# Five layer borders: the next layer's first two units of weights token-major behind the last product

## The chip, the cores and the metric

One of the cores of a Trainium2 chip runs the whole program, in one launch. The metric is the time of the program on the device in microseconds (us). The engines of a core have a queue each and run it in order: TensorE (PE: matmuls, PEld: its weight loads), VectorE (DVE), ScalarE (ACT), GpSimd (POOL), and SyncE (SP), which here issues the loads of weights.

## The reference, cut to what matters

A chain of layers over 256 tokens of width 1024, in fp32: two layers of mixers with a feed-forward each (the first dense, the second 8 experts of which a token takes 2), then forgetting attention, a conv FFN, a sparse attention, and another conv FFN. Each takes the normalised sum of all before it.

```python
h = rms_norm(x, norm_mix_g[layer]) * (1.0 + scale_m) + shift_m
... = jnp.split(h @ w_in[layer], split_points, axis=-1)      # four mixers
x = x + gate_m * mixed
h = rms_norm(x, norm_ffn_g[layer]) * (1.0 + scale_f) + shift_f
y = swiglu(h, w1, w3, w2)                                     # (silu(h @ w1) * (h @ w3)) @ w2
x = x + gate_f * y
...
def conv_ffn(xn, w_up, conv_w, conv_b, w_down):
    u = xn @ w_up
    c = sum((conv_w[j] * u_pad[:, j:j + T] for j in range(CONV_W)), conv_b)   # over tokens
    gate, val = jnp.split(c, 2, axis=-1)
    return (jax.nn.silu(gate) * val) @ w_down
```

## The kernel before, in words

**Products.** Every fp32 value is held as two parts, hi (rounded to fp32r) and lo (the rest); a product is three matmuls (mm3: hi·hi, lo·hi, hi·lo, lines L404 to L406). The features of a layer stand in hTh and hTl, feature-major: 8 pieces of 128 features by 256 tokens.

**Weights.** They come as a stream of units of 1 MB (`Stream`), in the order that `plan` writes down, 1024 x 256 or 256 x 1024 values each. SP loads a unit into one of 6 raw tiles; each half is split by a ScalarE cast (hi, L250) and a VectorE subtraction (lo, L251) into one of 4 split tiles, up to 3 halves ahead of their use. Some units are ada units: they are not split and belong to the modulation vectors of later layers. TensorE works through them in groups ("ada", "adt") that `fill` or `gap` puts in between, after the numbers in `FILL`.

**A unit of features.** `feat_unit` makes 256 new features by 256 tokens, 48 matmuls ("fu"). `tok_half` makes the same with tokens on the partitions, for 128 tokens at a time ("tu"), from a unit packed token-major; before, this is done for the first unit behind a border where the layer wants it so (mixers, forgetting and sparse attention).

**A border.** `close` is the last product of a layer: the output x, 256 tokens by 1024, in four quadrants (128 tokens tt by 512 columns n) of 12 matmuls each ("acc"). Behind each quadrant comes the residual (L1024 and L1025, with a gate at the first two borders, where GpSimd adds for tt = 0), the squares (L500), and behind the second one of each tt the norm (L428 to L435), the normalised rows xn (L487, or L492 and L490), their transposes on TensorE (`turned`, "tr", L447) and the features of the next layer (hTh by L468 or L473, hTl by L474). For tt = 0 this lies beside the second half of the last product. For tt = 1 TensorE runs 11 matmuls without a result behind the product (`warm`, L343) or, at the first two borders, an ada group, and then the transposes and the next layer's first units.

**Borders meant here.** B1: first mixers to dense FFN. B2: dense FFN to second mixers. B3: forgetting attention to conv FFN. B4: conv FFN to sparse attention. B5: sparse attention to conv FFN. (The border into the experts, `close_routed`, and the one out of them have code of their own.)

**FFN.** `gated_ffn` takes 11 pairs of units: for pair j a first and a second unit, then `pair` (swiglu, or the convolution over tokens and the gating: tile cf, 8 steps on VectorE, L1086 to L1094, then the split gh, gl), whose product with the down unit comes two pairs later.

## Time and profile before

| | |
|---|---|
| median of 3 runs | 2317.92 us (2312.59 to 2321.94) |
| profiled execution, its own time | 2317.72 us |
| its span, first to last instruction | 2315.6 us |
| PE busy | 2223.6 us (96%) |
| DVE busy | 1759.5 us (76%) |
| ACT busy | 1395.9 us (60%) |
| POOL busy | 90.3 us (4%) |
| mean granted clock of TensorE | 0.983 |

A share of busy time is a mean over stages. The experts take the middle of the span, from about 600 to 1590 us; the borders are short stretches at the ends of the other layers.

### The profile page before, as it was taken

To read this page: it belongs to the slowest core of one execution; us is meant where nothing else is said; L and a number is where in the kernel's file an instruction comes from. 1 tells how busy PE (TensorE), PEld (TensorE's weight loads), DVE (VectorE), ACT (ScalarE), POOL (GpSimd) and SP (SyncE) were. 2 spreads that over 40 slices of the span, in tenths; PEclk is the share of its full clock that TensorE was granted. 3 is DMA by queue.
4 is the path that set the end of the run, shared out by engine and by line. 5 is a ranking of instruction groups with operands and counts; after the bars stand their busy time and mean duration, and the time that the engine had idled before them with its cause. 6 is when DMAs were issued, how large, how long until landed. Compare 5 with 4: busy or idle time off the path is not lost. (4 is left out here: it accounts for less than half of the span.)

```text
span 2315.6 us, 34028 instructions
## 1 busy us (share of the span) xinstructions
PE 2223.6 (96%) x13353; PEld 1853.8 (80%) x13353; DVE 1759.5 (76%) x2279; ACT 1395.9 (60%) x1913; POOL 90.3 (4%) x118
## 2 busy tenths in 40 slices
PE   6998999899999999999999999898999998999999
PEld 4777888887887878787878878787879997778997
DVE  3665445586999899999999899886777776676776
ACT  3534334545777777777777777676655454455454
POOL 1000000001000000000000000001004001000000
PEclk8999999999999999999999999999999999999999
DMA  9757774635999999999999998794324544312542
GB/s 396 276 230 282 270 248 173 220 105 206 367 367 343 354 336 367 349 351 333 369 349 362 341 349 309 272 345 177 118 102 169 204 167 174 128 37 93 200 176 79
DMA packets 87559, 584.34 MB, mean 252 GB/s; under 512 B 9984, under 2 KB 11648, under 8 KB 20960
## 3 DMA queue, kind: packets, MB, share of 16 engines
q1 hardware_dynamic: 84096, 575.22, 67.2%
q0 software_dynamic: 1296, 4.59, 0.6%
q8 instruction: 106, 1.74, 0.3%
q10 hardware_dynamic: 2000, 2.29, 0.3%
q14 instruction: 61, 0.50, 0.1%
HBM read 580.76 MB, written 1.05 MB: 251 GB/s over the span
## 5 line engine op out<-in xcount | busy, mean ns | idle before, releaser
L251 DVE TENSOR_TENSOR lo<-raw,hi 128x1024 fp32r<-128x1024 f32 x711 | 853.2, 1227 | 280.7 <-ACT hi L250 274.0
L250 ACT CAST hi<-raw 128x1024 fp32r<-128x1024 f32 x718 | 740.2, 1049 | 356.8 <-PE fu L405 171.5
L404 PE MATMUL fu<-hTh,hi 128*128 128x256 f32 x1536 | 444.1, 289 | 4.4 <-DVE hTh L473 2.6
L406 PE MATMUL fu<-hTh,lo 128*128 128x256 f32 x1536 | 437.5, 285 | 2.2 <-DVE lo L251 2.2
L405 PE MATMUL fu<-hTl,hi 128*128 128x256 f32 x1536 | 437.8, 285 | 0.2 <-DVE hTl L474 0.2
L404 PE MATMUL h<-hi,xh 128*128 128x512 f32 x896 | 360.9, 403 | 6.2 <-DVEq L1418 6.0
L405 PE MATMUL h<-lo,xh 128*128 128x512 f32 x896 | 354.8, 396 | 4.6 <-DVE lo L251 4.6
L406 PE MATMUL h<-hi,xl 128*128 128x512 f32 x896 | 355.3, 397 | 0.0
L404 PEld LDWEIGHTS fu<-hTh,hi 128*128 128x128 f32 x1536 | 294.9, 192 | 21.3 <-issue 12.3
L405 PEld LDWEIGHTS fu<-hTl,hi 128*128 128x128 f32 x1536 | 293.3, 191 | 4.3 <-issue 3.2
L406 PEld LDWEIGHTS fu<-hTh,lo 128*128 128x128 f32 x1536 | 293.3, 191 | 2.8 <-DVE lo L251 2.8
L251 DVE TENSOR_TENSOR lo<-more,hi 128x1024 fp32r<-128x1024 f32 x216 | 258.3, 1223 | 21.4 <-ACT hi L250 19.7
L250 ACT CAST hi<-more 128x1024 fp32r<-128x1024 f32 x216 | 224.2, 1052 | 44.4 <-PE h L406 21.7
L405 PEld LDWEIGHTS h<-lo,xh 128*128 128x128 f32 x896 | 169.1, 189 | 45.6 <-DVE lo L251 7.9
L404 PEld LDWEIGHTS h<-hi,xh 128*128 128x128 f32 x896 | 168.9, 189 | 44.0 <-issue 6.4
L406 PEld LDWEIGHTS h<-hi,xl 128*128 128x128 f32 x896 | 168.8, 188 | 41.0
L404 PE MATMUL y<-hi,egh 128*128 128x512 f32 x448 | 177.1, 395 | 0.7 <-ACT egh L418 0.7
L406 PE MATMUL y<-hi,egl 128*128 128x512 f32 x448 | 177.6, 396 | 0.0
L405 PE MATMUL y<-lo,egh 128*128 128x512 f32 x448 | 176.5, 394 | 0.8 <-DVE lo L251 0.8
L404 PE MATMUL acc<-hi,gh 128*128 128x512 f32 x264 | 105.7, 400 | 0.0
L405 PE MATMUL acc<-lo,gh 128*128 128x512 f32 x264 | 104.7, 397 | 0.5 <-DVE lo L251 0.4
L406 PE MATMUL acc<-hi,gl 128*128 128x512 f32 x264 | 104.4, 396 | 0.0
(488 smaller groups left out, 2919.7 us busy)
## 6 DMA issues: line engine op xcount, KB each, us to landing
raw<-in_moe_dram SPq DMA_DIRECT2D x201, 1024.0 KB, 6.9
more<-in_moe_dram SPq DMA_DIRECT2D x108, 1024.0 KB, 7.0
raw<-in_w_ada_dram SPq DMA_DIRECT2D x48, 1024.0 KB, 6.8
raw<-in_f_up_dram SPq DMA_DIRECT2D x44, 1024.0 KB, 4.9
raw<-in_ffn_dram SPq DMA_DIRECT2D x33, 1024.0 KB, 5.2
row<-in_moe_dram SPq DMA_DIRECT2D x54, 512.0 KB, 7.0
raw<-in_w_in_dram SPq DMA_DIRECT2D x24, 1024.0 KB, 6.7
raw<-in_f_dn_dram SPq DMA_DIRECT2D x22, 1024.0 KB, 5.6
```

Of the source, the lines that this page charges most:

```text
L250: self.nc.scalar.copy(hi, src)
L251: (self.nc.gpsimd if pool else self.nc.vector).tensor_tensor(lo, src, hi.bitcast(FT), op=OP.subtract)
L404: t.matmul(out, a[0], b[0], start=start, stop=False)
L405: t.matmul(out, a[0], b[1], start=False, stop=False)
L406: t.matmul(out, a[1], b[0], start=False, stop=stop)
```

## The change

At the five borders, the first two units of the next layer are made token-major (`early=2`): their weights are packed that way on the host, and their four halves are split during the last product, into work tiles of the layer that ends (`spare`, `spares`) and not into the four split tiles. ScalarE casts all four when `close` starts; VectorE subtracts two ahead of the first residual, one after the second quadrant and one after the third. Behind the last product TensorE does the first 128 tokens of the first unit and of half of the second, then the transposes of tt = 1, the other half of the second unit, and after the features of tt = 1 both units for these. `warm` is gone there. hTl of tt = 0 now stands ahead of the last residual on VectorE. GpSimd takes no part in a border any more (residual, hTl, one split). At the first two borders two ada groups stand in the close, one behind the product and one ahead of the second 128 tokens; `FILL` takes them from other places, 40 groups in all as before. The FFNs and the sparse attention copy the token-major units they need feature-major (`tok_copy`, 2 ScalarE copies a unit) and turn them with 4 transposes a unit (`tok_turn`, "tt"); in an FFN, pair 0 is gated in the middle of pair 1. The second mixers use both as they are.

```diff
+    def spare(self, pairs):
...
+        rest = []
...
+            for t, src in zip(hi, raw):
+                self.nc.scalar.copy(t, src)
+            rest.append(lambda hi=hi, lo=lo, raw=raw: [
+                self.nc.vector.tensor_tensor(l, src, t.bitcast(FT), op=OP.subtract) for l, src, t in zip(lo, raw, hi)])
+            self.parts[self.cut] = (hi, lo)
+            self.spared.add(self.cut)
+            self.cut += 1
+        return rest
...
-    FILL = [1, 1, 1, 1, 1, 1, 1, 2, 2, 2, 2, 1], [3], [1] * 17 + [0] * 5, [3], [1] + [0] * 11
+    FILL = [1, 1, 1, 1, 1, 1, 1, 2, 2, 2, 2, 1], [2, 2], [0] * 2 + [1] * 16 + [0] * 4, [2, 2], [0] * 12
...
-        sub = v if tt or shift is None else nc.gpsimd
         def rest():
             if late:
                 v.tensor_copy(hi, tmp)
-            sub.tensor_tensor(lo, tmp, hi.bitcast(FT), op=OP.subtract)
+            v.tensor_tensor(lo, tmp, hi.bitcast(FT), op=OP.subtract)
...
-                if tt and n:
+                if n:
                     self.nc.vector.tensor_scalar(xn[:, s], self.x[:, tt, s], r, None, op0=OP.mult)
...
+    def spares(self, n):
+        r = []
+        for size, m in self.spare:
+            for _ in range(min(m, n - len(r))):
+                if size == 8192:
+                    t = self.w([P, 2, D], "sp", FR)
+                    r.append(([t[:, 0]], [t[:, 1]]))
+                else:
+                    r.append(tuple([self.w([P, size // 4], "sp", FR) for _ in range(4096 // size)] for _ in range(2)))
+        assert len(r) == n
+        return r
...
+        early = then[2] if then else 0
+        s = self.s
+        lows = s.spare(self.spares(2 * early))
+        def low(n):
+            for _ in range(min(n, len(lows))):
+                lows.pop(0)()
+        low(2)
         for tt in range(2):
             for n in range(2):
                 for i, (g, half, first, last) in enumerate(items):
                     if then and tt and n and i == m:
-                        rest = self.turned(0, rows[0][1], then)
+                        for f in self.turned(0, rows[0][1], then):
+                            f()
                     self.down_half(acc, g, half, first, last, tt, n)
                 self.residual(acc, gate, tt, n, rows[tt][1] if then else None)
                 if not then:
                     t, c = slice(tt * P, (tt + 1) * P), slice(n * 512, (n + 1) * 512)
                     self.nc.sync.dma_start(self.out[t, c], self.x[:, tt, c])
-                for f in rest:
-                    f()
                 if then:
                     self.summed(tt, rows[tt], n)
+                    if tt + n == 1:
+                        low(1)
+                    assert not (lows and tt and n)
             if then and tt == 0:
                 self.scaled(0, rows[0], then)
         if then:
             self.scaled(1, rows[1], then)
-            self.s.ahead(1, not (gap and then[2]))
-            if gap:
-                with self.s.quiet():
-                    gap()
-            else:
-                self.warm(11)
-            if then[2]:
-                self.s.ahead(2)
-            rest = self.turned(1, rows[1][1], then)
-            if then[2]:
-                with self.s.quiet():
-                    self.tok_half(0)
+            with s.quiet():
+                gap()
+                self.tok_half(0, 0)
+                if early > 1:
+                    self.tok_half(0, 1, (0,))
+                rest = self.turned(1, rows[1][1], then)
+                if early > 1:
+                    self.tok_half(0, 1, (1,))
+                gap()
             for f in rest:
                 f()
-            if then[2]:
-                self.tok_half(1)
-            else:
-                self.s.ahead(2)
+            s.ahead(4)
+            for u in range(early):
+                self.tok_half(1, u)
         return rows
...
-    def tok_half(self, tt):
+    def tok_half(self, tt, u=0, parts=(0, 1)):
         hi, lo = self.hT
-        if tt == 0:
-            self.first = [self.ps("tu"), self.ps("tu")]
-            self.firsts = [t.rearrange("p (k c) -> p k c", k=4) for h in self.s.halves(2) for t in h]
-            self.s.pinned = 2
-        s = slice(tt * P, (tt + 1) * P)
-        for j in range(8):
-            wh, wl = self.firsts[j // 4 * 2:][:2]
-            self.mm3(self.first[tt][:, :256], (hi[:, j, s], lo[:, j, s]), (wh[:, j % 4], wl[:, j % 4]), j == 0, j == 7)
+        s = self.s
+        if tt == 0 and 0 in parts:
+            if u == 0:
...
+            self.firsts.append((s.halves(2), held))
+            s.pinned += held
+            self.first.append([self.ps("tu"), self.ps("tu")])
+        halves, held = self.firsts[u]
+        t = slice(tt * P, (tt + 1) * P)
+        for h in parts:
+            wh, wl = ([p.rearrange("p (k c) -> p k c", c=256) for p in (w if isinstance(w, list) else [w])] for w in halves[h])
+            for k in range(4):
+                j = 4 * h + k
+                i, c = divmod(k, 4 // len(wh))
+                self.mm3(self.first[u][tt][:, :256], (hi[:, j, t], lo[:, j, t]), (wh[i][:, c], wl[i][:, c]), j == 0, j == 7)
         if tt:
-            self.s.pinned = 0
+            s.pinned -= held
+    def tok_copy(self, ps):
+        t = self.w([P, 2, 256], "tk")
+        for tt in range(2):
+            self.nc.scalar.copy(t[:, tt], ps[tt][:, :256])
+        return t
+    def tok_turn(self, t):
+        ps = self.ps("tt")
+        for m in range(2):
+            for tt in range(2):
+                self.nc.tensor.transpose(ps[:, (2 * m + tt) * P:(2 * m + tt + 1) * P], t[:, tt, m * P:(m + 1) * P],
+                                         self.cc("ident"))
+        return ps
...
-        (eng or (v if tt or gate is None else self.nc.gpsimd)).tensor_tensor(self.x[:, tt, s], t, self.x[:, tt, s], op=OP.add)
+        (eng or v).tensor_tensor(self.x[:, tt, s], t, self.x[:, tt, s], op=OP.add)
...
-        return (close or self.close)(acc, items, gate, then, gap)
-    def gated_ffn(self, pair, fill, gate, then, hT=None, gap=None):
-        acc = self.accs()
+        return close(acc, items, gate, then) if close else self.close(acc, items, gate, then, gap)
+    def gated_ffn(self, pair, fill, gate, then, hT=None, gap=lambda: None):
+        acc = None
         g = []
         n = 11
+        early = [self.tok_copy(ps) for ps in self.first]
         for j in range(n):
-            a = self.feat_unit()
+            if j == 0:
+                fill()
+                if len(early) == 2:
+                    fill()
+                    continue
+                b = self.feat_unit()
+                a = self.tok_turn(early.pop())
+            else:
+                a = self.feat_unit()
+                fill()
+                if early:
+                    g.append(pair(0, *map(self.tok_turn, early)))
+                    early = []
+                b = self.feat_unit()
             fill()
-            b = self.feat_unit()
-            fill()
+            if j == 2:
+                acc = self.accs()
             if j == n - 1:
                 g.append(pair(j, a, b))
...
-            nc.scalar.copy(vt[:, tt].rearrange("p b g d -> p (b g d)"), self.first[tt][:, :256])
-        ps = self.feat_unit()
+            nc.scalar.copy(vt[:, tt].rearrange("p b g d -> p (b g d)"), self.first[0][tt][:, :256])
         raw = self.w([P, 2, T], "raw")
-        nc.scalar.copy(raw.rearrange("p a t -> p (a t)"), ps)
+        nc.scalar.copy(raw.rearrange("p a t -> p (a t)"), self.tok_turn(self.tok_copy(self.first[1])))
...
-        self.phase("fox", c64=8, c1024=4, c1536=8, c2048=11, c8192=3)
-        self.forgetting(last, self.feats(self.row(a["fg"][0:1])))
+        self.phase("fox", c64=8, c1024=4, c1536=8, c2048=12, c8192=3, spare=((8192, 1), (2048, 3)))
+        self.forgetting(last, self.feats(self.row(a["fg"][0:1]), early=2))
...
-        ffn = dict(c64=8, c1024=4, c2048=20)
+        ffn = dict(c64=8, c1024=4, c2048=15, c8192=2, spare=((8192, 2), (2048, 2)))
         self.phase("cff0", **ffn)
-        rows = self.conv_ffn(0, self.feats(self.row(a["kvg"]), early=True), kT)
+        rows = self.conv_ffn(0, self.feats(self.row(a["kvg"]), early=2), kT)
...
-        self.phase("nsa", c64=12, c256=2, c512=6, c1024=7, c1536=3, c2048=12, c4096=3)
-        self.sparse(rows, self.row(a["bg"]), hT, self.feats(self.row(a["fg"][1:2])))
+        self.phase("nsa", c64=12, c256=2, c512=6, c1024=7, c1536=3, c2048=12, c4096=3, spare=((4096, 1), (2048, 3)))
+        self.sparse(rows, self.row(a["bg"]), hT, self.feats(self.row(a["fg"][1:2]), early=2))
```

On TensorE at B3, before: the rows from the last filler to the first unit (tr: transposes of the rows xn; fu: first unit, feature-major; identb: the filler's operand).

```order
L343 MATMUL warm_16703<-identb 128x512
L447 MATMUL tr_16715<-consts,xn_16608 128x128 x4
L447 MATMUL tr_16721<-consts,xn_16608 128x128 x4
L404 MATMUL fu_16752<-hTh,hi 128x256
L405 MATMUL fu_16752<-hTl,hi 128x256
L406 MATMUL fu_16752<-hTh,lo 128x256
```

After, around the same transposes (tu: second unit token-major for tt = 0; sp: its split weights in spare tiles):

```order
L440 MATMUL tu_16778<-sp_16637,hTh 128x256
L441 MATMUL tu_16778<-sp_16639,hTh 128x256
L442 MATMUL tu_16778<-sp_16637,hTl 128x256
L483 MATMUL tr_16792<-consts,xn_16630 128x128 x4
L483 MATMUL tr_16798<-consts,xn_16630 128x128 x4
L440 MATMUL tu_16778<-sp_16640,hTh 128x256
L441 MATMUL tu_16778<-sp_16642,hTh 128x256
L442 MATMUL tu_16778<-sp_16640,hTl 128x256
```

The transposes now follow 36 matmuls of the next layer instead of fillers, and are followed by 12 more that don't need their result.

On VectorE at B3, before, from the third quadrant's residual to the second half's rows:

```order
L1025 TENSOR_TENSOR x<-acc_16434,x 128x512
L502 TENSOR_SCALAR st_16607<-st_16607 128x1
L1025 TENSOR_TENSOR x<-acc_16435,x 128x512
L474 TENSOR_TENSOR hTl<-tr_16668,hTh 128x4x128
L474 TENSOR_TENSOR hTl<-tr_16674,hTh 128x4x128
L430 TENSOR_SCALAR rm_16690<-st_16607 128x1
L431 TENSOR_SCALAR rm_16690<-rm_16690 128x1
L434 SCALAR_TENSOR_TENSOR rm_16690<-rm_16690 128x1
L435 SCALAR_TENSOR_TENSOR st_16607<-rm_16690 128x1
L487 SCALAR_TENSOR_TENSOR xn_16608<-x,st_16607,row_15268 128x512 x2
```

After, the same place (L284: a split into a spare tile; L1103 is the residual, L509 hTl, L522 the rows):

```order
L1103 TENSOR_TENSOR x<-acc_16456,x 128x512
L537 TENSOR_SCALAR st_16629<-st_16629 128x1
L284 TENSOR_TENSOR sp_16642<-raw,sp_16640 128x512
L284 TENSOR_TENSOR sp_16643<-raw,sp_16641 128x512
L509 TENSOR_TENSOR hTl<-tr_16717,hTh 128x4x128
L509 TENSOR_TENSOR hTl<-tr_16723,hTh 128x4x128
L1103 TENSOR_TENSOR x<-acc_16457,x 128x512
L466 TENSOR_SCALAR rm_16739<-st_16629 128x1
L467 TENSOR_SCALAR rm_16739<-rm_16739 128x1
L470 SCALAR_TENSOR_TENSOR rm_16739<-rm_16739 128x1
L471 SCALAR_TENSOR_TENSOR st_16629<-rm_16739 128x1
L522 SCALAR_TENSOR_TENSOR xn_16630<-x,st_16629,row_15290 128x512 x2
```

A split and hTl of tt = 0 now stand ahead of the last residual; three more splits stand further ahead, around the first residuals.

On VectorE behind B5, before, the end of pair 0's gating and the start of pair 1's:

```order
L1088 SCALAR_TENSOR_TENSOR cf_20621<-fu_20555,vecs,cf_20621 128x254
L1094 TENSOR_TENSOR cf_20614<-cf_20614,cf_20621 128x512
L416 CAST gh_20630<-cf_20614 128x512
L419 TENSOR_TENSOR gl_20631<-cf_20614,gh_20630 128x512
L251 TENSOR_TENSOR lo<-raw,hi 128x1024 x4
L1087 SCALAR_TENSOR_TENSOR cf_20752<-fu_20634,vecs,cf_20752 128x255
L1088 SCALAR_TENSOR_TENSOR cf_20752<-fu_20634,vecs,cf_20752 128x254
```

After, the same two gatings (tt: units turned from token-major):

```order
L1180 SCALAR_TENSOR_TENSOR cf_20736<-tt_20724,vecs,cf_20736 128x254
L1186 TENSOR_TENSOR cf_20729<-cf_20729,cf_20736 128x512
L452 CAST gh_20745<-cf_20729 128x512
L455 TENSOR_TENSOR gl_20746<-cf_20729,gh_20745 128x512
L267 TENSOR_TENSOR lo<-raw,hi 128x1024 x2
L1179 SCALAR_TENSOR_TENSOR cf_20808<-fu_20662,vecs,cf_20808 128x255
L1180 SCALAR_TENSOR_TENSOR cf_20808<-fu_20662,vecs,cf_20808 128x254
```

Two splits instead of four stand between the two gatings.

## Rows read from the trace of the kernel before

**Rows 1.** The page, busy time by engine (share of the span, instructions)

```profile
PE 2223.6 (96%) x13353; PEld 1853.8 (80%) x13353; DVE 1759.5 (76%) x2279; ACT 1395.9 (60%) x1913; POOL 90.3 (4%) x118
```

**Rows 2.** Waits of PE, 164 to 200 us: us, times, longest

```profile
PE tr L447 <- ACT xn L492: 3.2, 2, 2.6
PE fu L404 <- DVE hTh L473: 2.6, 1, 2.6
```

**Rows 3.** Waits of PE, 400 to 432 us

```profile
PE tr L447 <- ACT xn L492: 3.3, 2, 2.6
PE tu L405 <- DVE lo L251: 2.7, 2, 1.8
PE adt L711 <- ACT xn L708: 0.7, 1, 0.7
```

**Rows 4.** Waits of PE, 1930 to 1960 us

```profile
PE tr L447 <- DVE xn L487: 3.3, 2, 2.0
PE fu L404 <- ACT hi L250: 1.4, 1, 1.4
PE fu L406 <- DVE lo L251: 0.8, 1, 0.8
```

**Rows 5.** Timeline of PE, 1730 to 1753 us: start, length, what

```profile
1731.79 2.55 PE L343 MATMUL warm<-identb 128*128 128x512 bf16 x11
...
1739.07 0.56 PE L404 MATMUL fu<-hTh,hi 128*128 128x256 f32 x1
...
1744.05 0.28 PE L406 MATMUL fu<-hTh,lo 128*128 128x256 f32 x1
...
1751.85 0.28 PE L405 MATMUL fu<-hTl,hi 128*128 128x256 f32 x1
```

**Rows 6.** Windows: length, busy us by engine, PEclk (granted clock), DMA share, GB/s

```profile
186.20:190.80 4.60, 4.36 (x19) 4.09 (x20) 4.60 (x5) 2.43 (x3) 0.18 (x1) 0.50 0.84 264
412.50:416.00 3.50, 3.50 (x17) 3.50 (x18) 3.47 (x8) 1.62 (x4) 0.00 (x0) 0.53 0.98 407
1941.70:1945.40 3.70, 3.70 (x21) 3.70 (x20) 1.90 (x3) 1.87 (x2) 0.12 (x1) 0.54 0.69 229
1951.80:1955.50 3.70, 3.67 (x18) 3.67 (x19) 3.38 (x3) 1.56 (x2) 0.00 (x0) 0.55 0.39 102
2119.00:2123.00 4.00, 4.00 (x23) 3.98 (x21) 2.98 (x4) 3.42 (x4) 0.00 (x0) 0.57 0.00 0
28.35:31.82 3.47, 0.01 (x1) 0.00 (x0) 2.15 (x8) 3.02 (x7) 0.97 (x1) 0.80 1.00 409
33.00:37.00 4.00, 3.75 (x17) 3.75 (x18) 4.00 (x7) 1.39 (x5) 4.00 (x10) 0.50 0.93 348
423.00:431.00 8.00, 6.20 (x48) 5.45 (x47) 7.03 (x7) 3.64 (x5) 0.00 (x0) 1.00 0.62 228
```

**Rows 7.** Groups of DVE instructions, 164 to 190 us

```profile
L251 DVE TENSOR_TENSOR lo<-raw,hi 128x1024 fp32r<-128x1024 f32 x5 | 5.8, 1217 | 0.0
```

**Rows 8.** Groups of DVE instructions, 2100-2119 us: busy, mean ns, idle

```profile
L487 DVE SCALAR_TENSOR_TENSOR xn<-x,st,row 128x512 f32<-128x512 f32 x4 | 4.9, 1272 | 0.1
L1025 DVE TENSOR_TENSOR x<-acc,x 128x512 f32<-128x512 f32 x4 | 2.8, 690 | 3.2 <-PE acc L406 3.2
```

**Rows 9.** Timeline of DVE, 2131 to 2156 us

```profile
2131.69 0.48 DVE L1087 SCALAR_TENSOR_TENSOR cf<-fu,vecs,cf 128x255 f32<-128x255 f32 x1
...
2139.60 4.62 DVE L251 TENSOR_TENSOR lo<-raw,hi 128x1024 fp32r<-128x1024 f32 x4
2144.15 0.48 DVE L1087 SCALAR_TENSOR_TENSOR cf<-fu,vecs,cf 128x255 f32<-128x255 f32 x1
...
2151.22 4.62 DVE L251 TENSOR_TENSOR lo<-raw,hi 128x1024 fp32r<-128x1024 f32 x4
```

**Rows 10.** Waits of PE, 1753 to 1790 us

```profile
PE fu L406 <- DVE lo L251: 1.4, 2, 1.1
```

**Rows 11.** The page, DMA issues: KB each, us to landing

```profile
raw<-in_f_up_dram SPq DMA_DIRECT2D x44, 1024.0 KB, 4.9
```

More of the change, by code (lines that the diff above doesn't have):

```diff
@@ L38, in _ts1024, with _first256 @@
     return w.reshape(-1, 2, P, D).transpose(0, 2, 1, 3).reshape(-1, P, 2048)
+def _first256(w, *units):
+    r = _ws(w)
+    for u in units:
+        r[u] = _ts256(w[:, u * 256:(u + 1) * 256])[0]
+    return r
 def _kcol(w):
@@ L192, in pack @@
     w = a["f_w_up_2"]
-    o["f_up"] = np.stack([_ws(w[l]) for l in range(2)])
+    o["f_up"] = np.stack([_first256(w[l], *EARLY_UP) for l in range(2)])
     o["f_dn"] = np.stack([_ts1024(a["f_w_down_2"][l]) for l in range(2)])
@@ L238, in split_to @@
     def split_to(self, n, pool=False):
-        n = min(n, self.SPLIT - self.pinned) - sum(self.across <= self.units[h // 2][1] for h in range(self.used, self.cut))
+        ahead = [h for h in range(self.used, self.cut) if self.across <= self.units[h // 2][1]]
+        n = min(n - len(ahead), self.SPLIT - self.pinned - sum(h not in self.spared for h in ahead))
         while n > 0 and self.cut < 2 * len(self.units):
-            u, h = divmod(self.cut, 2)
+            u = self.cut // 2
             if self.units[u][1]:
@@ L479, in turned, with feats @@
         return [then[1](tt, c, self.turn_rows(xn, c)) for c in range(2)]
-    def feats(self, gain, shift=None, early=False):
+    def feats(self, gain, shift=None, early=0):
         def rows(tt, r, xn, n):
@@ L525, in normed, with close @@
                 rest()
-            if then[2]:
-                self.tok_half(tt)
-    def close(self, acc, items, gate, then, gap=None):
+            for u in range(then[2]):
+                self.tok_half(tt, u)
+    def spares(self, n):
[8 more added lines that the diff above has]
+        assert len(r) == n
+        return r
+    def close(self, acc, items, gate, then, gap=lambda: None):
         rows = [self.rows() for _ in range(2)] if then else None
         m = len(items) // 2
-        rest = []
+        early = then[2] if then else 0
[5 more added lines that the diff above has]
+        low(2)
         for tt in range(2):
@@ L910, in whole @@
             return t
-        hi = tok(self.first, "hi_")
+        hi = tok(self.first[0], "hi_")
         fill()
-        av = tok(self.tok_unit(), "av_")
+        av = tok(self.first[1] if len(self.first) > 1 else self.tok_unit(), "av_")
         fill()
@@ L1024, in residual, with project @@
             v.tensor_tensor(t, acc[tt][n], gate[:, s], op=OP.mult)
-        (eng or (v if tt or gate is None else self.nc.gpsimd)).tensor_tensor(self.x[:, tt, s], t, self.x[:, tt, s], op=OP.add)
+        (eng or v).tensor_tensor(self.x[:, tt, s], t, self.x[:, tt, s], op=OP.add)
     def accs(self):
         return [[self.ps("acc") for _ in range(2)] for _ in range(2)]
-    def project(self, y, gate, then, order=range(8), between=lambda: None, acc=None, gap=None, close=None):
+    def project(self, y, gate, then, order=range(8), between=lambda: None, acc=None, close=None, gap=lambda: None):
         k0 = 8 - self.TAIL
@@ L1114, in routing, with close_routed @@
         return rows, weight, bias
-    def close_routed(self, acc, items, gate, mod, _):
+    def close_routed(self, acc, items, gate, mod):
         nc, v = self.nc, self.nc.vector
@@ L1512, in combined @@
         rows, junk = [], []
-        then = self.feats(None, early=True)
+        then = self.feats(None, early=1)
         def half(tt, n, eng):
@@ L1581, in v_unit @@
         def v_unit(u):
-            ps = self.first
+            ps = self.first[0]
             if u:
@@ L2170, in run @@
         self.setup()
-        first = self.normed(self.feats(self.gs[:, 0, 0], self.modc[:, 0, 0:8], True))
+        first = self.normed(self.feats(self.gs[:, 0, 0], self.modc[:, 0, 0:8], 1))
         ada = self.ada(0, 0)
@@ L2199, in between @@
                 next(g2, None)
-            rows = self.project(y, self.gate[l, 1], then, (2, 3, 0, 1, 6, 7, 4, 5), between, gap=None if l else fill,
-                                close=self.close_routed if l else None)
+            rows = self.project(y, self.gate[l, 1], then, (2, 3, 0, 1, 6, 7, 4, 5), between, gap=fill, close=self.close_routed if l else None)
             for g in (g1, g2):
@@ L2208, in run @@
             if l == 0:
-                self.phase("ffn0", c64=8, c2048=20, c4096=4)
-                self.gated_ffn(self.swiglu, fill, self.gate[0, 2], self.feats(self.gs[:, 1, 0], self.modc[:, 1, 0:8], True),
+                self.phase("ffn0", c64=8, c2048=16, c8192=4, spare=((8192, 4),))
+                self.gated_ffn(self.swiglu, fill, self.gate[0, 2], self.feats(self.gs[:, 1, 0], self.modc[:, 1, 0:8], 2),
                                gap=fill)
```

50 lines of the change are left out of this document (33 added, 17 removed).

## The prediction

> **What bounds the kernel now.** I read the page first: TensorE is busy 96% of the span, VectorE 76%, ScalarE 60%, GpSimd 4% [rows 1]. So only what TensorE does for nothing, waits for, or does at its lower clock can be won. Next came the waits of TensorE stretch by stretch: within the layers there are hardly any, and the same few stand at each border between layers. I number the five borders in order of time: B1 (around 175 us), B2 (405), B3 (1732), B4 (1935) and B5 (2113). Each has three kinds of loss:
>
> *Waits.* At B1 TensorE waits 3.2 us for the normalised rows that it is to transpose and 2.6 for the first operand after that [rows 2]. At B2 it waits 3.3 for rows, 2.7 for splits of weights and 0.7 in an ada group [rows 3]. At B4 it waits 3.3 for rows, then 1.4 and 0.8 for splits [rows 4]; B3 and B5 have the same row of 3.3.
>
> *Fillers.* At B3, B4 and B5 eleven matmuls without a result run for 2.55 us [rows 5].
>
> *Clock.* From 1739.07 to 1744.05, 23 f32 matmuls of 256 columns start, one per 0.217 us; from 1744.05 to 1751.85 there are 65, one per 0.120 [rows 5]. The granted clock tells the same: 0.50 to 0.57 (the level of 1.2 GHz, or just over it where a window catches the rise) just after a border, in windows at B1, B2, twice at B4, and B5 [rows 6]. So 1 - 0.120/0.217 = 0.45 of a slow stretch is lost; I take 0.44, as its first matmul is long without the clock: B1 4.6 us, lost 2.0; B2 3.5, 1.5; B3 5.0, 2.2; B4 3.7 and 3.5 (less at its ends), 1.6 and 1.5; B5 4.1, 1.8.
>
> What can be won is therefore: B1 3.2 + 2.6 + 0.2 (a short wait behind it, estimated) + 2.0 = 8.0; B2 3.3 + 2.7 + 0.7 + 1.5 = 8.2; B3 2.55 + 3.3 + 2.2 = 8.05; B4 2.55 + 3.3 + 1.4 + 0.8 + 1.6 + 1.5 = 11.15; B5 2.55 + 3.3 + 1.8 = 7.65. Together 43 us, of 2317.7.
>
> **What the change does to that.** Behind the last product TensorE no longer waits for the second 128 tokens: it has 36 matmuls of the first 128, at 0.120 each 4.3 us, then the transposes, then 12 more (1.45 us), and only then needs the second half's features. Before, the first piece of the second half's rows came 2.55 + 1.3 = 3.85 us after the last product (filler, and the first of two waits: 3.3 less the longest, 2.0 [rows 4]), and the other piece later. 4.3 us covers most of this, so fillers and long waits go. In their place come shorter waits, because VectorE now has more to do during the last product: four splits at 1.22 us [rows 7], 4.9 us, and at B1 and B2 the additions and the hTl that GpSimd did, at 0.69 each [rows 8].
>
> At B3 VectorE stood idle about 3.2 us for TensorE in such a close (the same group at B5, [rows 8]); 4.9 less 3.2 leaves it 1.7 us late. Counted forward, its queue then gives the first hTl of the first tokens at about 1733.9, while TensorE is through with the last product at 1732.2 (1731.79 [rows 5] and 0.4 of small waits for the first half's rows) and has two matmuls that can go without hTl, to 1732.5: a wait of 1.4. After this nothing is late: the last rows are out at about 1738.3, as the 36 matmuls end. Remaining waits: 0.4 + 1.4 = 1.75. B5 has the same queue without one of the small waits: 1.6. At B4 it is 1.6 too, and then about 1.9 before its transposes, since ScalarE's two copies of the raw unit stand behind other work in its queue; nothing if they don't. The four splits' ScalarE casts (an estimate of 4 to 5 us by the like shape of the split [rows 7]) lie under the last product, whose 48 matmuls of 512 columns outlast them.
>
> At B1 and B2 the residual costs VectorE two passes a piece, and the same count gives 3.35 at B1 (1.4 for the first half's rows, 0.9 and 0.45 for its features, 0.55 for the second half's rows) and 4.55 at B2 (0.3, 0.85, 0.45, 0.55, then 0.75 and 1.65 around the last ada group, whose gate matmuls and two VectorE products now stand inside the close). The ada groups placed there are real work that leaves other places: 40 before and after, so they count nothing.
>
> What the change adds on TensorE are transposes that turn the token-major units round: eight of 128x128 at B1, B3 and B5, 1.05 us; four at B4, 0.5. At B2 the units are used as they are.
>
> So the losses left are B1 3.35 + 1.05 = 4.4, B2 4.55, B3 1.75 + 1.05 = 2.8, B4 1.6 + 1.9 + 0.5 = 4.0, B5 1.6 + 1.05 = 2.65: 18.4 in all. Gain at the borders 43.05 - 18.4 = 24.65.
>
> **What comes back behind B3 and B5.** The gating of a pair of units in the conv FFN takes VectorE from 2131.69 to 2139.60, 7.9 us, the first time, and 2144.15 to 2151.22, 7.1, later, with four splits between [rows 9]. Before, a pair's gating fell beside 10 us of products of the next pair, and at B5 nothing waited. Now pair 0's units are turned late (in the middle of pair 1), so both gatings stand in VectorE's queue with only two splits between. For B5: before, the first two units end at about 2119.0 + 96 x 0.120 + 1.8 = 2132.3; now 7.65 - 1.6 us earlier, at 2126.3. Two halves of the third unit (48 matmuls, 5.8 us) go to 2132.1, the transposes to 2133.1; VectorE has pair 0 from about 2133.5 to 2141.4, then a split to 2142.6, while TensorE has run three halves more by 2141.8 (wait 0.8) and two more by 2148.4; VectorE's second split ends at 2143.8, pair 1 at 2150.9, the next split at 2152.1: a wait of 3.7. Together 4.5, at B5 and B3 alike; B3 loses its old 1.4 [rows 10]. Net cost 4.5 + 4.5 - 1.4 = 7.6. The swiglu pair at B1 is one pass and a split (under 2.2 us), and doesn't do this. Bounds: pair 1's ScalarE steps may run ahead of VectorE's pair 0, and its eight steps of 0.48 [rows 9], two passes at 0.69 and a cast (0.4, an estimate) then take 5.6 instead of 7.1 (each stall 1.5 less); or one more split or cast is late (1.2 more at each).
>
> A wait of 3.7 can also lower the clock. Idle of 3.47 us from 28.35 was followed by 0.50 from 33 to 37 [rows 6]. A single wait of 1.8 at B2 [rows 3] was not: the clock is 1.00 from 423 to 431 [rows 6]. This one lies just above the nearest row. I charge one drop of the two, 2.1 us (a mean slow stretch here, 4 to 5 us x 0.44).
>
> **Sum.** 24.65 - 7.6 - 2.1 = 15.0. The profiled execution took 2317.72 us, and the median of the three runs is 2317.92, so no shift: 2302.7.
>
> **Rivals.**
> *More is won (chance 0.22).* VectorE works the two gatings without ScalarE's gaps and the clock stays up: 24.65 + 1.4 - 2 x 3.0 = 20, perhaps 1.6 more at B4: about 2297. For it: ScalarE has 40% of its time free [rows 1]. Against: the gating took 7.1 where its passes are 5.6, so VectorE does wait within it now.
>
> *VectorE's queue becomes the close's bound (0.26).* The waits that I put at 0.4 to 1.4 grow, because the rows' product took 1.27 us on average, twice the other passes of its shape [rows 8]. GpSimd's split, which the change takes out of the close, may explain it; if it costs that without GpSimd too, two a border make the waits 1.2 us longer. B1 and B2 then have over 4.5 us of waits within some 10 us, enough for the clock to fall as it did behind 3.3 us of waits at every border now. Price: 5 x 1.2 + 3 x 2.1 = 12, gain about 3 to 8, so 2310 to 2315, no measurable change. Against: no single wait there exceeds 1.7.
>
> The Trainium skill, TensorE: Matmul & The Clock Gate, section "A second HAM failure mode: psum-queue depth-cycling", tells of a kernel whose short idles between groups of matmuls were enough to make the clock swing, and so speaks for this rival. By it every border would keep its slow stretch (2 us at each), a gain of some 7 instead of 15 (B4 had two). The single waits of up to 1.8 without a drop speak against it here [rows 3]; the borders of now, where two waits sum to 3.3 [rows 4], speak for it.
>
> *The change doesn't take (0.06).* The transposes stay the end of the chain, since the second half's rows come after the 4.3 us: gain only fillers and clock, 2306 to 2313.
>
> *Slower (0.06).* The four casts stand first in ScalarE's in-order queue at the close, and squares, means and features behind them. If the second unit's weights land late, the queue stops at the third cast and everything behind. Loads take 4.9 us in the median [rows 11], and in SP's queue those of the first units stand far ahead of each close. Only a wait of more than 15.0 / 5 = 3 us at each border turns the sign; with 4 at each it is 2317.7 - 15.0 + 20 = 2323.
>
> **How the numbers follow.** The likeliest is my sum with 0.40: 2302.7, its own range 2298 to 2308. The rivals put 2297 below, 2310 to 2315 above, and 2323 at the far end. I reach from 2293 to 2315, which leaves out the slower case and the tails of the others, about 2 in 10. A measurement of this kernel tells a change of about 0.5% (11.6 us) from none: faster means below 2306.3. Faster by that: 0.22 of the first rival, 0.36 of my case, 0.05 of the others, 0.63. Slower: 0.06. The same: 0.31.
>
> **What would show it.** In the changed profile: no filler at B3 to B5; waits of TensorE for rows under 1.5 us each; granted clock 1.0 after all five closes; a wait of 3 to 4 us for a split some 25 us behind the last product at B3 and B5, with the two gatings on VectorE before it; and, if I charge right, one slow stretch behind it. I am wrong if a slow stretch still follows the closes, if the wait behind the gatings is below 2 or above 6 us, or if a ScalarE cast waits for a load.

## The result, and the profile after

The changed kernel took 2294.31 us (median of 4 runs, 2291.86 to 2294.63), the kernel before beside it 2319.19 (4 runs): ratio 0.9895, 95% interval 0.9872 to 0.9917. It is faster by about 1%, some 24.5 us. The forecast was 2302.7, in a range of 2293 to 2315: right in direction and within the range, near its lower end, and the gain is some ten us larger than the forecast's 15.

The page after, its span and its line of busy times (before: [rows 1]): TensorE's busy time fell by 12 us and the span by 22.7, so about half of the gain is idle time, and half is work done at the full clock or not done (fillers).

```profile
span 2292.9 us, 34013 instructions
...
PE 2211.9 (96%) x13348; PEld 1846.7 (81%) x13348; DVE 1758.7 (77%) x2306; ACT 1398.3 (61%) x1934; POOL 65.3 (3%) x104
```

TensorE's waits after, in this order: three rows from 155 to 205 us (B1, [rows 2]), four from 380 to 435 (B2, [rows 3]), three from 1700 to 1770 (B3), two from 1900 to 1970 (B4, [rows 4]), three from 2070 to 2150 (B5). Columns are us in total, times, longest.

```profile
PE tr L483 <- ACT xn L527: 1.2, 2, 0.9
PE tu L440 <- DVE hTh L508: 0.6, 1, 0.6
PE tu L442 <- DVE hTl L509: 0.2, 1, 0.2
...
PE tu L440 <- DVE hTh L508: 1.6, 2, 1.1
PE adt L789 <- ACT xn L786: 0.7, 1, 0.7
PE tu L442 <- DVE hTl L509: 0.4, 2, 0.2
PE tr L483 <- ACT xn L527: 0.3, 1, 0.3
...
PE fu L442 <- DVE lo L267: 3.9, 2, 2.7
PE fu L440 <- ACT hi L266: 1.1, 1, 1.1
PE tu L442 <- DVE hTl L509: 1.0, 1, 1.0
...
PE tu L442 <- DVE kTl L509: 1.0, 1, 1.0
PE tt L668 <- ACT tk L660: 0.9, 1, 0.9
...
PE fu L442 <- DVE lo L267: 2.7, 2, 2.2
PE tu L442 <- DVE hTl L509: 0.9, 1, 0.9
PE fu L440 <- ACT hi L266: 0.9, 1, 0.9
```

Single waits of 2 to 2.6 us in the closes have become waits of 0.2 to 1.1. New are the waits of a product for a split (fu for lo and hi): behind B3 5.0 us with the cast, where there were 1.4 [rows 10], and behind B5 3.6, where there were none.

Windows after (length, busy us by engine, granted clock, DMA share, GB/s), the closes of B1 and B2 and the stretches behind the new waits at B3 and B5 [rows 6]:

```profile
178.00:190.00 12.00, 10.93 (x93) 8.09 (x86) 9.42 (x23) 6.92 (x14) 0.53 (x1) 1.00 0.86 319
404.00:415.00 11.00, 8.63 (x59) 5.30 (x58) 5.40 (x15) 7.42 (x12) 0.00 (x0) 1.00 0.79 313
1758.30:1763.00 4.70, 4.64 (x21) 4.64 (x22) 3.61 (x4) 0.00 (x0) 1.38 (x3) 0.50 0.76 275
2128.30:2132.50 4.20, 4.17 (x22) 4.17 (x23) 3.38 (x3) 0.12 (x1) 0.00 (x0) 0.60 0.74 257
```

The closes now run at the full clock in spite of their short waits (the same view gives 1.00 from 1718 to 1735, 1920.6 to 1944 and 2089.4 to 2110, behind the last products of B3, B4 and B5); where the waits for splits stand, the clock is at its lower level (0.50 is 1.2 GHz) for as long as one stood at a border before.

The lead of the changed kernel over the kernel before, by the start of the same thing on TensorE in the two profiled executions, shows where the time came from:

| what starts | before | after | lead | won since | forecast |
|---|---|---|---|---|---|
| behind B1's last product (ada) | 177.22 | 177.02 | 0.2 | | |
| fillers ahead of the dense FFN's last product | 389.93 | 383.77 | 6.2 | B1 6.0 | 3.6 |
| narrow projection behind B2 (nr) | 442.98 | 431.59 | 11.4 | B2 5.2 | 3.65 |
| behind B3's last product | 1731.79 | 1718.08 | 13.7 | 2.3 | 0 |
| first down product of the first conv FFN | 1777.77 | 1763.22 | 14.55 | B3 0.8 | 2.15 |
| behind B4's last product | 1934.81 | 1920.66 | 14.15 | -0.4 | 0 |
| narrow projection behind B4 (nr) | 1967.40 | 1944.61 | 22.8 | B4 8.65 | 7.15 |
| behind B5's last product | 2112.17 | 2089.49 | 22.7 | -0.1 | 0 |
| first down product of the second conv FFN | 2155.30 | 2132.53 | 22.8 | B5 0.1 | 0.5 |

(The forecast's column has the losses before less those left, at B3 and B5 less the waits for splits; the one clock drop that it charged, 2.1, is not in it.) B1, B2 and B4 carry the gain; B3 and B5 won in the close and had given it back by the first down product, 45 and 43 us behind the last product.

### The profile page after: what moved, and what is told of

It is laid out like the page before. It is cut to its first block, busy times and chain, and to the rows that moved or that the text cites. A ratio compares the mean times of both kernels' runs of the same rounds, so it can differ in the third digit from the quotient of the medians.

```text
span 2292.9 us, 34013 instructions
## 1 busy us (share of the span) xinstructions
PE 2211.9 (96%) x13348; PEld 1846.7 (81%) x13348; DVE 1758.7 (77%) x2306; ACT 1398.3 (61%) x1934; POOL 65.3 (3%) x104
## 5 line engine op out<-in xcount | busy, mean ns | idle before, releaser
L267 DVE TENSOR_TENSOR lo<-raw,hi 128x1024 fp32r<-128x1024 f32 x695 | 831.3, 1223 | 274.7 <-ACT hi L266 267.6
L266 ACT CAST hi<-raw 128x1024 fp32r<-128x1024 f32 x698 | 719.4, 1049 | 343.9 <-PE fu L441 164.2
L440 PE MATMUL fu<-hTh,hi 128*128 128x256 f32 x1440 | 414.9, 288 | 3.9 <-ACT hi L266 1.9
L442 PE MATMUL fu<-hTh,lo 128*128 128x256 f32 x1440 | 410.5, 285 | 7.4 <-DVE lo L267 7.4
L441 PE MATMUL fu<-hTl,hi 128*128 128x256 f32 x1440 | 409.5, 284 | 0.0
L440 PEld LDWEIGHTS fu<-hTh,hi 128*128 128x128 f32 x1440 | 276.1, 192 | 19.9 <-issue 12.2
L442 PEld LDWEIGHTS fu<-hTh,lo 128*128 128x128 f32 x1440 | 273.8, 190 | 8.4 <-DVE lo L267 8.4
L441 PEld LDWEIGHTS fu<-hTl,hi 128*128 128x128 f32 x1440 | 274.2, 190 | 3.2 <-issue 2.2
L266 ACT CAST hi<-more 128x1024 fp32r<-128x1024 f32 x216 | 224.2, 1052 | 44.2 <-PE h L442 22.7
```

The lines of the kernel that those rows point to most:

```text
L266: self.nc.scalar.copy(hi, src)
L267: (self.nc.gpsimd if pool else self.nc.vector).tensor_tensor(lo, src, hi.bitcast(FT), op=OP.subtract)
L440: t.matmul(out, a[0], b[0], start=start, stop=False)
L441: t.matmul(out, a[0], b[1], start=False, stop=False)
L442: t.matmul(out, a[1], b[0], start=False, stop=stop)
```

## The experiments

Each kernel was timed beside the kernel before; ratios are to that. The first four ran on one chip, where the kernel before had a median of 2318.51.

**Pair 0 gated right behind the border.** In the two conv FFNs:

```diff
                 if len(early) == 2:
                     fill()
+                    if soon:
+                        g.append(pair(0, *map(self.tok_turn, early)))
+                        early = []
                     continue
...
```

> In the two conv FFNs pair 0's token-major units are turned and gated right behind the border, not in the middle of pair 1; all else as in the changed kernel. Theory (both gatings stand in VectorE's queue with two splits between, and the stall lowers the clock): the waits of 1.2 + 1.1 + 2.7 us behind B3 and 0.5 + 0.9 + 2.2 behind B5 go, and with them the slow stretch behind each (about 2 us); a new wait of some 0.4 us for ScalarE's last copy comes ahead of the transposes. 2294.3 - 5.0 - 3.6 - 4.0 + 0.8 = about 2282.5. Rival (the turned units come late because of ScalarE's copies and casts, or the splits wait for tiles, wherever the gating stands): the same waits move or stay, 2291 to 2295.

2279.72 us (2277.35 to 2282.14, 5 runs), ratio 0.9834 (0.9819 to 0.9848). TensorE's waits in this kernel, 1700 to 1770 us and then 2075 to 2150:

```profile
PE fu L442 <- DVE lo L267: 1.4, 1, 1.4
PE tu L442 <- DVE hTl L509: 1.0, 1, 1.0
...
PE tu L442 <- DVE hTl L509: 0.9, 1, 0.9
```

The waits for splits are gone behind B5 and down to 1.4 behind B3; the new wait of 0.4 that the theory allowed for does not show. The reason is the place of the gatings on VectorE. After the change, behind B5 (first step of pair 0; the splits behind it; first step of pair 1; the splits behind it):

```profile
2109.79 0.48 DVE L1179 SCALAR_TENSOR_TENSOR cf<-tt,vecs,cf 128x255 f32<-128x255 f32 x1 [1.74 <-ACT cf L1178]
...
2117.72 2.36 DVE L267 TENSOR_TENSOR lo<-raw,hi 128x1024 fp32r<-128x1024 f32 x2
2119.99 0.48 DVE L1179 SCALAR_TENSOR_TENSOR cf<-fu,vecs,cf 128x255 f32<-128x255 f32 x1
...
2127.06 4.62 DVE L267 TENSOR_TENSOR lo<-raw,hi 128x1024 fp32r<-128x1024 f32 x4
```

And in this kernel:

```profile
2094.83 0.48 DVE L1182 SCALAR_TENSOR_TENSOR cf<-tt,vecs,cf 128x255 f32<-128x255 f32 x1 [1.91 <-ACT cf L1181]
...
2102.75 3.49 DVE L267 TENSOR_TENSOR lo<-raw,hi 128x1024 fp32r<-128x1024 f32 x3
2106.15 0.47 DVE L1182 SCALAR_TENSOR_TENSOR cf<-fu,vecs,cf 128x255 f32<-128x255 f32 x1
...
2113.22 4.62 DVE L267 TENSOR_TENSOR lo<-raw,hi 128x1024 fp32r<-128x1024 f32 x4
```

After the change both gatings lie between 2109.8 and 2127.1 with two splits between. Here pair 0 starts 15.0 us sooner by the clock on the wall, of which 9.2 is this kernel's lead there: 5.8 us, the products of the third unit that it no longer waits for (48 at 0.120). Three splits follow it instead of two, and from 2095 to 2112 TensorE does not wait. From behind the last product to the first down product TensorE takes 38.8 us at B3 (before this edit 45.1) and 37.4 at B5 (43.0): 6.4 and 5.7 won, 12.1 of the 15.0 between the two profiled executions. The theory holds. Most of the rest, 3.2 us, lies in the sparse attention, which the edit does not touch (told with the fourth split, below).

**Fillers in the wait.** The changed kernel with nine matmuls without a result where TensorE waits for the split:

```diff
+                if soon and j == 2:
+                    b = self.ps("fu")
+                    self.feat_mm(b[:, :T], self.s.half())
+                    h = self.s.half()
+                    self.warm(9)
+                    self.feat_mm(b[:, T:], h)
...
```

> The changed kernel with nine matmuls without a result (about 2.1 us) in the two conv FFNs where TensorE waits longest for a split, ahead of the last half of the third pair. Theory (the stall itself lowers the clock, which costs about 2 us behind each of B3 and B5): the waits are as long as before, partly filled, the granted clock behind them stays near 1.0, and 2 to 4 us are won: about 2291. Rival (the slow stretch has another cause, or the fillers' share is too small to hold the clock): clock as before, 2294 to 2296.

2292.81 us (2291.5 to 2293.38, 4 runs), ratio 0.9891 (0.9875 to 0.9906); the changed kernel has 0.9895. The windows that hold the end of the longest wait, or stand behind it, at B3 and B5, in the order of the columns above:

```profile
1758.00:1763.00 5.00, 3.41 (x25) 3.30 (x26) 5.00 (x5) 1.78 (x3) 2.82 (x4) 1.00 0.51 152
...
2128.50:2132.50 4.00, 4.00 (x24) 3.42 (x23) 2.79 (x3) 1.11 (x2) 0.00 (x0) 1.00 1.01 414
```

The granted clock stays at 1.00, where it was 0.50 and 0.60. Of the waits 3.3 us are left at B3 and 1.9 at B5, the longest 2.1 and 1.4. The kernel with GpSimd put back (next) has the waits of the changed kernel unfilled, 2.7 and 2.2 at the longest, and behind them the clock is 0.50 and 0.63 again. So in two executions without fillers the clock fell at both borders, and in one with them at neither, which speaks for the wait as what lowers it; it is no proof, because one and the same wait of 1.8 us is seen with and without a fall behind it (last section). In time the two stretches take 2.1 and 1.7 us less than after the change (table below). In the medians only 1.5 us shows and the intervals cover each other, so that the 2 to 4 us expected are neither shown nor excluded.

**GpSimd back at the gated borders.** The changed kernel with the residual's addition and hTl of the first 128 tokens on GpSimd, and hTl in the first norm of the program:

```diff
-        (eng or v).tensor_tensor(self.x[:, tt, s], t, ...
+        (eng or (v if tt or gate is None else self.nc.gpsimd)).tensor_tensor(self.x[:, tt, s], t, ...
...
+        sub = v if tt or shift is None else nc.gpsimd
...
-            v.tensor_tensor(lo, tmp, hi.bitcast(FT), op=OP.subtract)
+            sub.tensor_tensor(lo, tmp, hi.bitcast(FT), op=OP.subtract)
```

> The changed kernel with GpSimd back at the two gated borders and in the first norm: it does the residual's addition and hTl for the first 128 tokens, as before the change. Theory (GpSimd's passes take about 1.3 us against 0.69 on VectorE and slow VectorE's passes beside them; VectorE's queue has room without it): waits at B1 and B2 grow by 1 to 3 us each, 2296 to 2300. Rival (VectorE's queue is what the remaining waits at B1 and B2 hang on, so relieving it of four passes a border helps): 2291 to 2293.

2302.25 us (2297.82 to 2304.87, 6 runs), ratio 0.9927 (0.9913 to 0.9941) against 0.9895 (0.9872 to 0.9917): 7 to 8 us slower than the changed kernel, with intervals that just touch (and 9 slower than the fillers' kernel beside it, whose interval lies clear). That is on the theory's side and more than the 2 to 6 expected; 1.7 of it is a wait far from the borders, told below. Its waits at B1 (155 to 205 us; one row) and B2 (385 to 440):

```profile
PE tr L483 <- ACT xn L529: 2.3, 1, 2.3
...
PE tu L440 <- DVE hTh L510: 1.7, 2, 1.1
PE tr L483 <- ACT xn L529: 1.6, 1, 1.6
PE tu L442 <- POOL hTl L511: 0.9, 1, 0.9
```

And GpSimd's passes at B1:

```profile
L511 POOL TENSOR_TENSOR hTl<-tf,hTh 128x512 fp32r<-128x512 f32 x2 | 3.0, 1511 | 7.6 <-DVE hTh L510 7.6
L1105 POOL TENSOR_TENSOR x<-xn,x 128x512 f32<-128x512 f32 x2 | 3.0, 1478 | 55.6 <-DVE xn L1104 55.6
```

The first half's rows come late (2.3 and 1.6 us, against 0.9 and none after the change), and at B2 TensorE waits 0.9 for GpSimd itself. At B1 the other waits are gone, so that the sum grows by only 0.3 us there, less than the theory's 1 to 3; but behind the 2.3 the granted clock is 0.50 from 178.8 to 182.2, where it was 1.00. At B2 the sum grows from 3.0 to 5.1. A pass takes GpSimd 1.5 us on average, where VectorE takes 0.69 for the same shape [rows 8].

**The old border at B3 and B5.** The changed kernel with no early units at those two:

```diff
-EARLY_UP = (0, 11)
+EARLY_UP = ()
...
+            if not early:
+                self.first = []
+                s.ahead(1, True)
+                self.warm(11)
+                for f in self.turned(1, rows[1][1], then):
+                    f()
+                s.ahead(2)
+                return rows
...
```

> The changed kernel with the old border at B3 and B5 (first units feature-major behind the last product, eleven fillers, one split on GpSimd), the new one at B1, B2 and B4. Theory (by the trace B3 and B5 win 6 to 8 us in the close and give all but 0.5 us back behind it): about 2294.8, no measurable difference. Rival (the border's gain there is real and the loss behind it belongs to something that happens anyway): slower by 6 to 13 us, 2300 to 2307.

2292.24 us (2290.25 to 2296.9, 5 runs), ratio 0.9894 (0.9878 to 0.991). No difference from the changed kernel that shows, as the theory has it: at B3 and B5 the change brings nothing on balance. The old border's low clock is back there (0.50 from 1725.8 to 1729 and from 2092 to 2096) instead of the one behind the gatings.

From behind the last product to the first down product, in us, in the profiled executions:

| kernel | B3 | B5 |
|---|---|---|
| before | 46.0 | 43.1 |
| changed | 45.1 | 43.0 |
| changed, pair 0 gated right behind the border | 38.8 | 37.4 |
| changed, fillers in the wait | 43.0 | 41.3 |
| changed, old border at B3 and B5 | 45.1 | 44.2 |
| before, without GpSimd at the borders (last experiment) | 44.9 | 40.7 |

So the early units are worth something at B3 and B5 only together with the early gating: the first experiment's kernel is 12.5 us faster than this one by the medians, and takes 13.3 less in these two stretches.

**The fourth split later.** The first experiment's kernel, with the last of the four early splits moved on VectorE from behind the third quadrant to behind the last one:

```diff
-                    if tt + n == 1:
+                    if n:
                         low(1)
```

> The kernel with pair 0 gated right behind the border, and besides at all five borders the fourth early split moved on VectorE from behind the third quadrant to behind the last one, where VectorE idles 0.8 us for the squares. Theory (the waits left in the closes hang on the length of VectorE's queue ahead of hTl of the first tokens): TensorE's waits for hTl, 1.0, 1.0 and 0.9 us at B3, B4 and B5, and 0.6 + 0.2 at B1 and 0.5 + 0.2 at B2, go, while nothing behind the last residual is late: 2279.7 - 3 to 4 = 2276. Rival (ScalarE's hTh and not VectorE's queue is what the wait hangs on, or the second half's rows then come 1.3 us later and TensorE waits for them instead): 2279 to 2282.

2281.38 us (2278.51 to 2281.79, 4 runs), ratio 0.9854 (0.9838 to 0.987) on another chip, where the kernel before had 2313.64. The wait for the first hTl, at B3 and at B4:

```profile
PE tu L442 <- DVE hTl L509: 0.2, 1, 0.2
...
PE tu L442 <- DVE kTl L509: 0.2, 1, 0.2
```

The waits fell from 1.0 to 0.2 as the theory says, and at B3 to B5 nothing behind became late (at B1 and B2 TensorE waits about 0.2 us longer for the second half's rows). The time did not fall: by ratio this kernel and the first experiment's can't be told apart. The profiled executions show what stands against it. Here are 100 us of the sparse attention between B4 and B5, which the edit does not touch, in this kernel and then in the first experiment's:

```profile
1960.00:2060.00 100.00, 93.25 (x663) 72.98 (x661) 65.64 (x193) 53.87 (x177) 6.95 (x17) 0.93 0.14 50
```

```profile
1962.00:2062.00 100.00, 93.23 (x690) 74.17 (x690) 67.03 (x197) 58.08 (x189) 7.41 (x18) 0.98 0.13 48
```

The mean granted clock was 0.93 here and 0.98 there, and TensorE started 663 matmuls instead of 690. From the narrow projection behind B4 to the end of the sparse attention's last product this kernel took 145.9 us and the first experiment's 141.4, 4.5 less, which is more than the waits won. The same stretch took 141.4 with the old border at B3 and B5 and 144.5 to 144.7 in the other five kernels, before and after among them. So it varies by 4.5 us between single executions, and the edit need have no part in it; whether it has was not settled.

**One part alone: no GpSimd.** The kernel before, with GpSimd's additions, hTl and split at the borders on VectorE, and nothing else of the change:

```diff
-        sub = v if tt or shift is None else nc.gpsimd
+        sub = v
...
-            self.s.ahead(1, not (gap and then[2]))
+            self.s.ahead(1)
...
-        (eng or (v if tt or gate is None else self.nc.gpsimd)).tensor_tensor(...
+        (eng or v).tensor_tensor(...
```

> The kernel before with one part of the change alone: GpSimd's additions, hTl and early split at the borders go to VectorE; units, fillers and ada groups as before. Theory (most of the gain is the token-major units, which fill the waits; GpSimd's part only shortens VectorE's and the residual's passes in the close): 2312 to 2318, the waits of 3.2 + 2.6 at B1 and 3.3 + 2.7 at B2 still there, within 1.5 us of what they were. Rival (GpSimd's slow passes and their weight on VectorE are the cause of most of the loss at the borders, as the kernel with GpSimd put back, 8 us slower, may be read): 2303 to 2308. Besides: the wait at the branch within the experts was 6.0 us in the kernel before and 5.9 with GpSimd put back, 4.1 to 4.2 in the four without GpSimd at the gated borders; if GpSimd's instructions there decide it, it is 4.2 here, and if not, 6.0.

2307.77 us (2304.51 to 2312.92, 6 runs), ratio 0.9969 (0.9956 to 0.9981) on the chip where the kernel before had 2313.64: about 7 us won by ratio (4 to 10), 6 by the medians. On the first chip that would be about 2311, between the theory's range and the rival's and nearer to the theory's. Its waits, in an execution that was the slowest of the six, at B1 (164 to 200), B2 (400 to 432), B4 (1930 to 1960), and at the branch within the experts:

```profile
PE fu L404 <- DVE hTh L473: 2.7, 1, 2.7
PE tr L447 <- ACT xn L492: 2.0, 1, 2.0
...
PE tu L405 <- DVE lo L251: 2.5, 2, 1.8
PE tr L447 <- ACT xn L492: 2.1, 1, 2.1
...
PE tr L447 <- DVE xn L487: 1.3, 1, 1.3
...
PE h L404 <- PEq L1418: 4.3, 1, 4.3
```

Against [rows 2 to 4] the wait for rows fell from 3.2 to 2.0, 3.3 to 2.1 and 3.3 to 1.3 (at B3 and B5 from 3.3 to 1.4 and 1.3); those for hTh and for splits hardly moved. So "within 1.5 us of what they were" held at B1 and B2, which it named, and not at B4. In this execution nothing was won in the stretches at B1 and B2 (212.8 and 54.2 us against 212.7 and 53.1 before, with a second stretch of low clock at B2), but 1.1, 3.0 and 2.4 at B3, B4 and B5, where GpSimd's only part was the split, and 1.7 at the branch. So both the theory (the part is small) and the rival (the slow passes at the gated borders are the cause) missed the place: most of what GpSimd costs in this execution is what its split did to VectorE's rows (last section). Of the change's 24.5 us about 7 can be had by GpSimd's part alone. The other 17 were not taken apart between the token-major units, the new order on VectorE and the places of the ada groups. The forecast had no term for the first.

## Why the prediction was right, and where its sizes were off

**What is won at the borders: right, sized too small.** The forecast left 3.35 us of waits at B1, 4.55 at B2 and 1.6 + 1.9 at B4. The rows after show 1.2 + 0.6 + 0.2 = 2.0, 1.6 + 0.7 + 0.4 + 0.3 = 3.0 and 1.0 + 0.9. That is 1.35, 1.55 and 1.6 less, against 2.4, 1.55 and 1.5 more won than forecast: it explains B2 and B4, and more than half of B1. The term mis-sized is "the same count gives 3.35 at B1 and 4.55 at B2", a walk along VectorE's queue: at B1 its parts 1.4, 0.9, 0.45 and 0.55 came as 0.9, 0.6, 0.2 and 0.3, and at B2 0.75 and 1.65 around the last ada group came as 0.7 and 1.3. Which passes on VectorE it took too long is not shown. At B3 and B5 the first hTl was waited for 1.0 and 0.9, not 1.4.

**What comes back behind B3 and B5: right.** Forecast 0.8 + 3.7 = 4.5 at each; measured 5.0 at B3 and 3.6 at B5, with both gatings on VectorE ahead of the split, as forecast: behind B5 they took 7.9 and 7.1 us, the forecast's own figures. In its pieces the sum is partly luck: the waits for splits were 1.2 and 2.7 at B3 and 0.5 and 2.2 at B5, so that the long one stayed below the 3 to 4 us named as the sign, and the wait for a ScalarE cast (1.1 and 0.9) stood in the forecast only as a bound. The long wait ends 40 and 39 us behind the last product; the "some 25 us" of the sign does not agree with the forecast's own count either, which puts it at 36 to 40 (2148.4 to 2152.1, against 2112.2). Gating pair 0 sooner took all but 1.4 us away, and undoing the two borders cost nothing.

**The clock.** One drop was charged for the two waits; both came (0.50 and 0.60 above), and fillers in the wait kept the clock up. That term was short by about 2 us. In the closes the granted clock is 1.00, with waits of up to 1.1 us between groups of matmuls. The Trainium skill, TensorE: Matmul & The Clock Gate, section "A second HAM failure mode: psum-queue depth-cycling", which tells of a swing of the clock caused by short idles between groups of matmuls, spoke for a low clock there; this did not happen here, so the measurement decides against it for this case.

**What the forecast had no term for.** Between B2 and B3 the lead grows by 2.3 us in code that the change leaves alone. 1.8 of it is the branch within the experts (the other 0.5 is not accounted for): TensorE's wait there, before, after, and with GpSimd put back:

```profile
PE h L404 <- DVEq L1418: 6.0, 1, 6.0
```

```profile
PE h L440 <- PEq L1510: 4.2, 1, 4.2
```

```profile
PE h L440 <- DVEq L1512: 5.9, 1, 5.9
```

It was 6.0 and 5.9 in the two kernels with GpSimd at the gated borders, and 4.1 to 4.3 in the six without. Two edits moved it, both GpSimd's alone: putting it back into the changed kernel, and taking it out of the kernel before (4.3). The traces narrow it down: TensorE's own branch instruction takes 6.1 to 6.2 us in every kernel; what differs is VectorE, whose work behind the branch comes late in the two kernels with GpSimd. Before:

```profile
1459.27 1.29 DVE L1316 TENSOR_TENSOR yt<-yt,row 128x512 f32<-128x512 f32 x2 [4.35 <-DVEq L1418]
```

After the change the same two products start 0.15 us behind the instruction ahead of them. VectorE also has fewer instructions ahead of the branch where GpSimd takes some (1850 and 1855 in the records, against 1860 or 1861), so it may be the place of the branch in VectorE's program that counts and not GpSimd. Why VectorE comes late stays open.

**The rivals.** *More is won* has the nearest time (2297), but not its reason: the gatings were not shorter and the clock did fall. *VectorE's queue becomes the close's bound* rested on the rows' product at 1.27 us. That is a mean of three products of 0.75 and one of 2.83 (last section); after the change both of the second half take 0.75. *The change doesn't take* and *slower* have nothing for them: the second half's transposes follow the 36 matmuls with 0.3 us of wait or none, and no cast of the early splits shows among what TensorE waits for.

**In sum.** On the forecast's own terms, with what the rows after show: left in the closes and for transposes (0.8 us for eight) 2.85 at B1, 3.0, 1.8, 2.4 and 1.7 at B5, 11.75 instead of 18.4; the waits behind B3 and B5 5.0 + 3.6 - 1.4 = 7.2 instead of 7.6; two drops of 2.1 instead of one. 43.05 - 11.75 - 7.2 - 4.2 = 19.9, where the table has 20.75 for the five borders, and 2.3 at the branch: 22 to 23, as the spans tell. The way was right; what is left in the closes was sized half too large (18.4 for 11.75), and the branch was not seen.

## What to carry to other kernels

A wait at a border can be filled with the next layer's own products, on the half of its input that is ready: at B3 and B5, with the early gating, that was 12.5 us better than the old border with its fillers and GpSimd's split. When work is made sooner, make its consumers sooner too: here the units came early and their gating late, two gatings then met in one queue, and both borders' gain went into the wait behind them until the gating was moved up as well (2279.7 us). A helper engine's pass has to be priced with what it does to its neighbour: taking GpSimd out of the kernel before was worth about 7 us, with VectorE busy 76% of the span with it and without. And a mean over four passes can hide the one that matters.

## What the runs showed of the hardware

VectorE's product of two operands in SBUF (the rows, 128x512) took 0.75 us by itself and 2.83 where it started while GpSimd was at a split; the 1.27 of [rows 8] is the mean of four. At B5 before, VectorE's first pair, its second pair and GpSimd's split:

```profile
2108.40 1.42 DVE L487 SCALAR_TENSOR_TENSOR xn<-x,st,row 128x512 f32<-128x512 f32 x2
...
2115.11 3.50 DVE L487 SCALAR_TENSOR_TENSOR xn<-x,st,row 128x512 f32<-128x512 f32 x2
...
2115.39 2.68 POOL L251 TENSOR_TENSOR lo<-raw,hi 128x1024 fp32r<-128x1024 f32 x1 [16.07 <-ACT hi L250]
```

The product that started within the split (2115.78) ended 0.5 us after it. It was the same at B3 and B4 (2.84 and 2.83), and TensorE's second wait for rows, 2.0 us at each of the three borders, follows it. In the kernel before without GpSimd the second pair at B5 took 1.41. The Trainium skill, GPSIMD Engine Reference, section "8. Key points", says that GpSimd shares its interfaces to SBUF with VectorE and names instructions with two inputs there as the ones that contend; the rows agree.

The clock's fall was not the same for the same instructions. In the sparse attention TensorE waits 1.8 us for the same VectorE instruction, in an order that no edit touched. The ten us from just ahead of that wait, before and then after:

```profile
2063.60:2073.60 10.00, 9.03 (x65) 6.99 (x66) 6.17 (x19) 3.65 (x11) 0.71 (x2) 1.00 0.19 44
```

```profile
2038.00:2048.00 10.00, 9.24 (x40) 7.65 (x40) 4.21 (x9) 3.35 (x10) 1.73 (x2) 0.66 0.21 61
```

The granted clock was 1.00 before and 0.66 after. Behind this wait it fell to 0.50 in four of the eight profiled executions (after, fillers, GpSimd put back, and the kernel before without GpSimd) and stayed at 1.00 in the other four. Likewise the wait of 1.8 at B2, behind which the forecast's row shows 1.00, was followed by 0.50 (428.6 to 432) in the kernel before without GpSimd. Some 3 us hang on this, in either direction, in a single execution, so a difference of that size between two profiled executions is not yet one between two kernels.
